# Keeping the first norm's token tiles in on-chip memory through the memory attention

## The chip, the cores and the metric

The kernel runs on one core of a Trainium2 chip. Its engines work side by side, each on its own list of instructions, in the order of that list: TensorE (in the profile PE; its weight loads PEld) multiplies matrices, VectorE (DVE) and ScalarE (ACT) do element-wise work and may read the accumulators of TensorE, GpSimd (POOL) does element-wise work between on-chip buffers, and SyncE (SP) issues nearly all transfers between the on-chip memory and the main memory. The metric is the device time of one execution, in microseconds, smaller being better.

## The reference

One layer of an encoder over 1024 tokens of width 1024, with three sub-layers, each closed by a residual and a layer norm. What the kernel must compute is `h`, with `DEPTH = 1`:

```
h = layer_norm(x, ln_in_w, ln_in_b)
h = layer_norm(ALPHA * h + hybrid_mixer(h, ...), ln1_w, ln1_b)       # first norm
h = layer_norm(ALPHA * h + memory_xattn(h, mem, ...), ln2_w, ln2_b)  # memory attention
h = layer_norm(ALPHA * h + conv_ffn(h, ...), ln3_w, ln3_b)
```

The mixer is an mLSTM over half of the width and a neighbourhood attention over the other half, with a common output projection. The memory attention lets every token attend, in 4 heads, to 256 memory rows: scores of the token with the keys, a softmax for each head, the sum of the values, an output projection and a bias `b_xo`. The last sub-layer is a gated convolutional feed-forward network.

## The kernel before

Tokens are worked in 8 tiles of 128 tokens by 1024 columns, 512 KB in fp32, 4,096 bytes in each of the 128 partitions. Products are made exact enough by splitting each operand into a high and a low part, and each product is three matmuls (`mm3`, lines 225 to 227).

The change lies at the seam between the mixer and the memory attention.

*The end of the mixer* (`out_half`, line 1061, called at 1309). `part0` in main memory holds, for each tile, ALPHA times the residual plus one half of the output projection plus the bias. For each tile, in the order `todo = [0, 2, 1, 3, 4, 6, 5, 7]`, `load_r` fetches these rows into a buffer `r` of the pool `wkB`, which has five (line 1071); TensorE makes the other half of the projection in two accumulators; VectorE adds them to `r` (line 1090, twice). Then `after1` (line 1295) normalizes the tile in place: statistics on VectorE (lines 238 to 242), the power -1/2 on GpSimd (line 243), a shift on VectorE (line 252), the scaling on ScalarE (line 253), times `ln1_w` on VectorE (line 1297), plus `ln1_b` on GpSimd (line 1298), and a store to `h_1` in main memory (line 1299). A tile's statistics are held behind the shift of the tile before (`hold`). `ln1_w` and `ln1_b` lie in the buffers vec0 and vec1. For the first two tiles `to_hT` (line 1265) makes the transposed fp16 halves that TensorE takes: a split on ScalarE and VectorE into `h1s` (two buffers), and two transposing transfers on SyncE into `h1T` (two buffers, line 1270).

*The memory attention*, again tile by tile. `load_r` (line 1380) fetches the tile from `h_1` into one of five buffers of the pool `rtiles`, which lies at the upper end of the on-chip memory; `to_hT` follows for the third tile on, and GpSimd adds `b_xo` to the tile (lines 1438 and 1447). `scores` (line 1385) makes the 48 matmuls of the scores (keys and query projection are already multiplied into one matrix) and the softmax into the halves `Ps`; `to_PT` (line 1410) transposes these by two transfers on SyncE (line 1415) into vec0 for even and vec1 for odd tiles (vec2 for the last); `out_d` (line 1418) makes the 48 matmuls with values and output projection, adds them to the tile (line 1426), normalizes and stores it, and `to_B` (line 1324) transposes it for the feed-forward network. The loop at line 1440 has `scores` of tile n+1, `to_PT` of n, `load_r` and `to_hT` of n+2, and `out_d` of n-1.

The order in which each engine gets its instructions is not the order of the program: a planner that simulates the time of each instruction writes the lists (`schedule_with_timeline_sim=True`), and puts the semaphores between them. Pools opened later may take the space of pools closed earlier; an instruction then waits for the last user of the tiles that it overlaps (`reuse_waits="tile"`). At the lower end of the on-chip memory the program keeps a scratch for transfers issued by GpSimd, 16,384 bytes in each partition unless it is told otherwise.

Of the kernel before, what the change touches and what calls it, by code (L numbers as in the profile page):

```python
# [8 lines left out]
F32 = mybir.dt.float32  # L9
# [8 lines left out]
D = 1024  # L18
SEQ = 1024
MEM = 256  # L20
NT = 8
FF = 2816
NFF = FF // 128
ALPHA = 2.0 ** 0.25
# [26 lines left out]
def run(gen):  # L51
    for _ in gen:
        pass
# [3 lines left out]
def encoder(ctx, tc, I, out):  # L57
    nc = tc.nc
    V, A, G, T, S = nc.vector, nc.scalar, nc.gpsimd, nc.tensor, nc.sync
# [19 lines left out]
    def bank(name):  # L79
        key = "mem" if name == "tk" else name  # L80
        turn[key] = turn.get(key, -1) + 1
        tag = SET[name][turn[key] % len(SET[name])]
        return pp.tile([128, 512], F32, name=name, tag=tag, bufs=NB[tag])
# [4 lines left out]
    def dscratch(name, shape, dt=F32):  # L88
        return dram.tile(shape, dt, name=name)

    h0_d = dscratch("h_0", [SEQ, D])
    part0_d = dscratch("part0", [SEQ, D])
    h1_d = dscratch("h_1", [SEQ, D])
    part1_d = dscratch("part1", [SEQ, D])
    h2_d = dscratch("h_2", [SEQ, D])
    mo_d = dscratch("mo", [SEQ, 512])
# [70 lines left out]
    def col(n=1):  # L167
        used[0] += n
        assert used[0] <= 96
        return sc[:, used[0] - n:used[0]]  # L170
# [32 lines left out]
    def split16(hi, lo, src, s):  # L203
        A.activation(hi, src, AF.Copy, scale=s)  # L204
        return V.scalar_tensor_tensor(lo, src, s, hi, op0=OP.mult, op1=OP.subtract)  # L205
# [11 lines left out]
    def slot(tag):  # L217
        return (xp.tile([128, 4096], F32R, name=tag + "h", tag=tag + "h"),
                xp.tile([128, 4096], F32R, name=tag + "l", tag=tag + "l"))
# [4 lines left out]
    def mm3(ps, lh, ll, rh, rl, first, last, skip=False):  # L224
        T.matmul(ps, lh, rh, start=first, stop=False, skip_group_check=skip)  # L225
        T.matmul(ps, lh, rl, start=False, stop=False, skip_group_check=skip)  # L226
        return T.matmul(ps, ll, rh, start=False, stop=last, skip_group_check=skip)  # L227
# [54 lines left out]
    with ExitStack() as ca:  # L282

        yml = None
        with ExitStack() as cm:
# [258 lines left out]
            with ExitStack() as c2:  # L544
# [256 lines left out]
                with ExitStack() as c1:  # L801
# [10 lines left out]
                    for c in range(4):  # L812
                        w, ic = cw[2 + c]
# [244 lines left out]
            return [wload(I[wname][(k0 + k) * 128:(k0 + k + 1) * 128, :], 1, 1024, engs[k], raws[k])  # L1058
                    for k in range(4)]

        def out_half(w, y, res, dst, work, name, after=None, bias=None, rbufs=3, early=False, alpha=ALPHA, todo=range(NT)):


            rs = {}

            def load_r(tt):
                if tt == 0 and early:
                    rs[tt] = wp.tile([128, WP], F32, name="wraw", tag="wraw", bufs=2)[:, :D]
                else:
                    rs[tt] = work.tile([128, D], F32, name="r", tag="r", bufs=rbufs)  # L1070
                S.dma_start(rs[tt], res[tt * 128:(tt + 1) * 128, :])

            load_r(todo[0])
            yield 0
            for n, tt in enumerate(todo):
                if n + 1 < NT:
                    load_r(todo[n + 1])
                r = rs.pop(tt)
                for ch in range(2):
                    ps = bank(name)  # L1080
                    for k in range(4):
                        yh, yl = y(k, tt)
                        wh, wl = w[k]
                        cc = slice(ch * 512, ch * 512 + 512)
                        mm3(ps, yh, yl, wh[:, 0, cc], wl[:, 0, cc], k == 0, k == 3)
                    rc = r[:, ch * 512:ch * 512 + 512]
                    if bias is not None:
                        V.scalar_tensor_tensor(rc, rc, alpha, ps, op0=OP.mult, op1=OP.add)
                    else:
                        V.tensor_tensor(rc, ps, rc, OP.add)  # L1090
                    yield 1
                if bias is not None:
                    G.tensor_tensor(r, r, bias, OP.add)
                if dst is not None:
                    S.dma_start(dst[tt * 128:(tt + 1) * 128, :], r)
                if after is not None:
                    yield from after(tt, r)

        wA = out_w("w_mix_out", 0, (None, V, None, V))
        yna = tuple(t.rearrange("p (k t) -> p k t", k=4) for t in slot("X2"))  # L1100

        with ExitStack() as cn:
# [109 lines left out]
            def ylk(y):  # L1212
                return lambda k, tt: (y[0][:, k, tt * 128:(tt + 1) * 128], y[1][:, k, tt * 128:(tt + 1) * 128])

            wB = []
# [17 lines left out]
    with ExitStack() as cb_:  # L1233
# [26 lines left out]
        todo = [0, 2, 1, 3, 4, 6, 5, 7]  # L1260
        rs, hT, probs, rq, holds, stores = {}, {}, {}, [], [], []
        cC = ExitStack()
        ck = cC.enter_context(tc.tile_pool(name="wkC", bufs=1, reuse_waits="tile"))

        def to_hT(ck, n, r):
            hT[n] = ck.tile([128, 2, 8, 128], F16, name="h1T", tag="h1T", bufs=2)
            hl = ck.tile([128, 2, D], F16, name="h1s", tag="h1s", bufs=2)
            split16(hl[:, 0], hl[:, 1], r, s1)
            for i in range(2):
                S.dma_start_transpose(hT[n][:, i], hl[:, i])  # L1270

        with ExitStack() as cB:
            wk = cB.enter_context(tc.tile_pool(name="wkB", bufs=1, reuse_waits="tile"))
            lw, lb = vec(0, "ln1_w"), vec(1, "ln1_b")
            p1, s1 = pow2(ln_bound(lw, lb)[1], 14)

            cs_, ncs = col(), col()
            V.tensor_scalar(cs_, p1, scales["q"][0], 2.0 ** -23, op0=OP.mult, op1=OP.mult)
            V.tensor_tensor(cs_, cs_, pk, OP.mult)
            V.tensor_scalar(ncs, cs_, -1.0, None, op0=OP.mult)  # L1280
            bxo = vec(2, "b_xo")

            wb2 = small.tile([128, 16], F32, name="wb2")
            S.dma_start(wb2, I["ln2_c"])
            bup = small.tile([128, 2 * NFF], F32, name="bup")
            S.dma_start(bup, I["b_up"])
            m2 = col(3)
            V.tensor_reduce(m2[:, 0:1], wb2[:, 0:8], axis=mybir.AxisListType.X, op=OP.max, apply_absolute_value=True)
            V.tensor_reduce(m2[:, 1:2], wb2[:, 8:16], axis=mybir.AxisListType.X, op=OP.max, apply_absolute_value=True)
            V.scalar_tensor_tensor(m2[:, 2:3], m2[:, 0:1], float(D) ** 0.5, m2[:, 1:2], op0=OP.mult, op1=OP.add)  # L1290
            ph, sh = scale_of(m2[:, 2:3], 12)
            V.tensor_scalar(wb2, wb2, sh, None, op0=OP.mult)
            holds = []

            def after1(tt, r):
                holds.append(ln_tile(r, None, None, small, hold=holds[-1] if holds else None))
                V.tensor_tensor(r, r, lw, OP.mult)
                G.tensor_tensor(r, r, lb, OP.add)
                S.dma_start(h1_d[tt * 128:(tt + 1) * 128, :], r)
                if tt in todo[:2]:  # L1300
                    first.append(r)
                    if tt == todo[1]:
                        to_hT(ck, 0, first[0])
                if tt == todo[4]:
                    to_hT(ck, 1, first[1])
                yield 1

            first = []
            run(out_half(wB, ylk(yna), part0_d, None, wk, "out", after1, rbufs=5, todo=todo))

        rtx = ExitStack()
        rt = rtx.enter_context(tc.tile_pool(name="rtiles", bufs=1, side="right", reuse_waits="tile"))

# [61 lines left out]
        Bop["B22"] = tuple(wp.tile([128, 2048], F16, name=t, tag=t, bufs=5).rearrange("p (k t) -> p k t", k=4)  # L1377
                           for t in ("whi", "wlo"))

        def load_r(n):  # L1380
            if n < NT:
                rs[n] = rt.tile([128, D], F32, name="r", tag="r", bufs=5)
                S.dma_start(rs[n], h1_d[todo[n] * 128:todo[n] * 128 + 128, :])

        def scores(ck, n):
            t = hT.pop(n)
            P = ck.tile([128, D], F32, name="P", tag="P", bufs=1)
# [46 lines left out]

        V.tensor_scalar(bxo, bxo, 1.0 / ALPHA, None, op0=OP.mult)
        for n in range(2):
            load_r(n)
            G.tensor_tensor(rs[n], rs[n], bxo, OP.add)
        P = scores(ck, 0)
        for n in range(NT - 1):  # L1440
            Pn = scores(ck, n + 1)
            to_PT(P, n)
            P = Pn
            if n + 2 < NT:
                load_r(n + 2)
                to_hT(ck, n + 2, rs[n + 2])
                G.tensor_tensor(rs[n + 2], rs[n + 2], bxo, OP.add)
            if 0 < n < NT - 2:
                run(out_d(n - 1))
# [26 lines left out]
        class Units:  # L1476
# [26 lines left out]
            def home(self, v):  # L1503
                i = v % 4
                if i not in homes:
                    homes[i] = (lambda: in_yp("Yh"), in_ur, lambda: in_yp("Yl"), in_wp)[i]()
                return homes[i]
# [88 lines left out]
        with ExitStack() as cE:  # L1596
            wk = cE.enter_context(tc.tile_pool(name="wkE", bufs=1, reuse_waits="tile"))
# [182 lines left out]
        with ExitStack() as cF:  # L1780
            wk = cF.enter_context(tc.tile_pool(name="wkF", bufs=1, reuse_waits="tile"))
# [12 lines left out]
            for j in range(1, 5):  # L1794
                for tt in range(NT):
# [3 lines left out]
                    if tt in (0, 4) and j < 4:  # L1799
                        f = 4 * j + 4 + tt // 2  # L1800
# [19 lines left out]
            rs = {}  # L1820
# [9 lines left out]
            for tt in range(NT):  # L1830
                load_r(tt + 2)
                r = rs.pop(tt)
# [8 lines left out]
                n = 256 if last else 512  # L1841
# [95 lines left out]
```

## Time and profile before

| | |
|---|---|
| median of 3 runs | 1527.25 us (1524.54 to 1528.09) |
| the profiled execution | 1526.06 us |
| its span | 1524.1 us |
| its mean granted TensorE clock | 0.985 |
| TensorE busy | 1447.8 us |
| VectorE, ScalarE, GpSimd busy | 1033.7, 825.6, 574.5 us |
| moved between the memories | 217.00 MB |
| transfers of tiles between `h` scratches and `r` buffers | 19 loads and 16 stores of 512 KB |

All lines below are of the one profiled execution. Its order of time gives, for each instruction, the start in us from the beginning of the span, the duration, the engine, the line of the kernel, the operation, output and inputs by the names of the tiles, the count where neighbours are merged, and in brackets the time for which the engine stood idle before it, with what ended that. SPq is SyncE's queue: its rows are the issues of transfers, not the transfers. A line can be that of a helper (225 to 227 are all matmuls of split products, 204 and 205 all splits), so tiles tell the stage: `out` is the end of the mixer, `S` the scores and the outputs of the memory attention.

### The profile page before, as it was taken

Reading aid. Unit: us, or ns where it says so; the run is one execution under the profiler, and the core shown is the slowest. Engines: PE = TensorE matmul, PEld = TensorE weight load, DVE = VectorE, ACT = ScalarE, POOL = GpSimd, SP = SyncE. Lnnn points to the kernel's source line nnn. Section 1 sums busy time; section 2 is a strip of 40 time slices with the busy share of each in tenths; the row PEclk is TensorE's granted clock in tenths of the full one; section 3 lists DMA queues with packets and bytes.
Section 4 is the critical chain, followed back from the end, with each engine's and each line's share of the span. In section 5 each row is a group of like instructions: output and inputs, shape, how many; then the busy total and the mean of one; then the engine's idle time right before and its main releaser. Section 6 shows DMA issues by size and latency. Waiting matters only on the chain. (4 is left out here: it accounts for less than half of the span.)

```text
span 1524.1 us, 21708 instructions
## 1 busy us (share of the span) xinstructions
PE 1447.8 (95%) x8060; PEld 869.3 (57%) x8060; DVE 1033.7 (68%) x1945; ACT 825.6 (54%) x1393; POOL 574.5 (38%) x453
## 2 busy tenths in 40 slices
PE   8999999999999898994999979999999999999998
PEld 6998776466666887861444434444444444444444
DVE  7868866536776678565456778887787779807434
ACT  5765565654544666323444758777777767503000
POOL 5442367204326766044013374434443420300543
PEclk9999999999999999997999989999999999999999
DMA  8846563315446534476333342323222436712111
GB/s 305 325 157 218 178 194 137 96 50 153 130 133 191 184 105 152 188 221 166 89 77 85 126 152 111 111 111 124 112 111 111 152 124 221 264 54 86 53 74 65
DMA packets 118687, 217.00 MB, mean 142 GB/s; under 512 B 40883, under 2 KB 69811, under 8 KB 115254
## 3 DMA queue, kind: packets, MB, share of 16 engines
q1 hardware_dynamic: 118288, 214.86, 42.3%
q8 instruction: 63, 1.03, 0.3%
q0 software_dynamic: 144, 0.49, 0.2%
q14 instruction: 42, 0.34, 0.1%
q10 hardware_dynamic: 150, 0.27, 0.0%
HBM read 158.34 MB, written 49.35 MB: 136 GB/s over the span
## 5 line engine op out<-in xcount | busy, mean ns | idle before, releaser
L1527 POOL TENSOR_TENSOR wraw<-ur 128x512 f32<-128x512 f32 x22 | 45.9, 2086 | 207.7 <-issue 192.4
L226 PE MATMUL dn<-wlo,yp 128*128 128x512 f16 (+1 forms) x284 | 105.1, 370 | 0.0
L225 PE MATMUL dn<-whi,yp 128*128 128x512 f16 (+1 forms) x284 | 104.9, 370 | 0.0
L227 PE MATMUL dn<-whi,yp 128*128 128x512 f16 (+1 forms) x284 | 104.4, 370 | 0.0
L1615 DVE SCALAR_TENSOR_TENSOR cbuf<-C,wdw,cbuf 128x1024 f32<-128x1024 f32 x44 | 69.9, 1588 | 35.3 <-ACT cbuf L1614 35.1
L227 PEld LDWEIGHTS <-wlo 128*128 128x128 f16 x540 | 52.8, 98 | 56.6 <-DVE wlo L205 1.3
L226 PEld LDWEIGHTS <-whi 128*128 128x128 f16 x540 | 52.9, 98 | 56.0 <-issue 3.2
L225 PEld LDWEIGHTS <-whi 128*128 128x128 f16 x540 | 52.9, 98 | 53.2 <-ACT whi L204 0.3
L243 POOL TENSOR_TENSOR lnrs<-lnrs,mhalf 128x1 f32<-128x1 f32 x32 | 24.8, 775 | 138.5 <-DVE lnrs L242 132.8
L205 DVE SCALAR_TENSOR_TENSOR wlo<-wraw,us,whi 128x1024 f16<-128x1024 f32 (+1 forms) x48 | 62.7, 1324 | 18.7 <-ACT whi L204 18.7
L253 ACT ACTIVATE r<-r,lnrs 128x1024 f32<-128x1024 f32 x19 | 23.6, 1240 | 88.1 <-DVE lnrs L252 88.0
L1616 DVE SCALAR_TENSOR_TENSOR cbuf<-C,wdw,cbuf 128x1024 f32<-128x1024 f32 x44 | 70.4, 1600 | 0.7
L225 PE MATMUL S<-whi,vec 128*128 128x512 f16 x128 | 49.3, 385 | 15.6 <-DMA vec<-Ps 15.6
L204 ACT ACTIVATE whi<-wraw,us 128x1024 f16<-128x1024 f32 (+1 forms) x48 | 51.2, 1103 | 16.5 <-DVE us L177 15.6
L1614 ACT ACTIVATE cbuf<-C,bdw,wdw 128x1024 f32<-128x1024 f32 x44 | 54.2, 1234 | 8.9 <-DVE C L1652 8.4
L226 PEld LDWEIGHTS <-yp 128*128 128x128 f16 x370 | 36.2, 98 | 39.9
L225 PEld LDWEIGHTS <-yp 128*128 128x128 f16 x370 | 36.2, 98 | 39.8
L227 PEld LDWEIGHTS <-yp 128*128 128x128 f16 x370 | 36.2, 98 | 39.7
L225 PE MATMUL tk<-whi,Bo 128*128 128x256 f16 (+1 forms) x192 | 53.3, 277 | 1.6 <-DVE stage L205 1.6
L227 PE MATMUL tk<-whi,Bo 128*128 128x256 f16 (+1 forms) x192 | 53.3, 278 | 0.0
L226 PE MATMUL tk<-wlo,Bo 128*128 128x256 f16 (+1 forms) x192 | 53.3, 278 | 0.0
L226 PE MATMUL tk<-wlo,Be 128*128 128x256 f16 (+1 forms) x192 | 52.4, 274 | 0.9 <-DVE wlo L205 0.9
(520 smaller groups left out, 4898.7 us busy)
## 6 DMA issues: line engine op xcount, KB each, us to landing
ur<-in_w_up_dram SPq DMA_DIRECT2D x22, 1024.0 KB
sv<-in_w_down_dram SPq DMA_DIRECT2D x22, 512.0 KB
y<-cbuf SPq DMA_DIRECT2D x22, 512.0 KB
ur<-y SPq DMA_DIRECT2D x11, 1024.0 KB
wraw<-in_w_down_dram SPq DMA_DIRECT2D x22, 512.0 KB
r<-h SPq DMA_DIRECT2D x19, 512.0 KB
h<-r SPq DMA_DIRECT2D x16, 512.0 KB
wraw<-in_w_tok_dram SPq DMA_DIRECT2D x10, 512.0 KB
```

Source lines behind the costliest of these rows:

```text
L204: A.activation(hi, src, AF.Copy, scale=s)
L205: return V.scalar_tensor_tensor(lo, src, s, hi, op0=OP.mult, op1=OP.subtract)
L225: T.matmul(ps, lh, rh, start=first, stop=False, skip_group_check=skip)
L226: T.matmul(ps, lh, rl, start=False, stop=False, skip_group_check=skip)
L227: return T.matmul(ps, ll, rh, start=False, stop=last, skip_group_check=skip)
L243: G.tensor_tensor(rs[:, 0:1], rs[:, 0:1], mhalf[:, 0:1], OP.pow)
L253: A.activation(r, r, AF.Identity, scale=rs[:, 0:1], bias=rs[:, 1:2])
L1527: G.tensor_tensor(S1, A21, A22, OP.add)
L1614: A.activation(c, C[:, 1:SEQ + 1], AF.Identity, scale=wdw[:, 1, j:j + 1], bias=bdw[:, j:j + 1])
L1615: V.scalar_tensor_tensor(c, C[:, 0:SEQ], wdw[:, 0, j:j + 1], c, op0=OP.mult, op1=OP.add)
L1616: V.scalar_tensor_tensor(c, C[:, 2:SEQ + 2], wdw[:, 2, j:j + 1], c, op0=OP.mult, op1=OP.add)
```

## The change

Eight tiles `r0` to `r7` of the pool `rtiles`, which is now opened before the end of the mixer, take the rows of `part0` (`home`). They are normalized there, and the memory attention works on the same tiles. The store to `h_1`, the loads from it, `h_1` itself and the pool `wkB` go. The third to eighth tile's `to_hT` stays where it was in the program. The scratch for transfers issued by GpSimd is made 4,096 bytes a partition.

```diff
-    h1_d = dscratch("h_1", [SEQ, D])
...
-        def out_half(w, y, res, dst, work, name, after=None, bias=None, rbufs=3, early=False, alpha=ALPHA, todo=range(NT)):
+        def out_half(w, y, res, dst, work, name, after=None, bias=None, rbufs=3, early=False, alpha=ALPHA, todo=range(NT), home=None):
...
                 if tt == 0 and early:
                     rs[tt] = wp.tile([128, WP], F32, name="wraw", tag="wraw", bufs=2)[:, :D]
+                elif home is not None:
+                    rs[tt] = home(tt)
                 else:
                     rs[tt] = work.tile([128, D], F32, name="r", tag="r", bufs=rbufs)
                 S.dma_start(rs[tt], res[tt * 128:(tt + 1) * 128, :])
...
+        rtx = ExitStack()
+        rt = rtx.enter_context(tc.tile_pool(name="rtiles", bufs=1, side="right", reuse_waits="tile"))
+
+        def home(tt):
+            n = todo.index(tt)
+            rs[n] = rt.tile([128, D], F32, name=f"r{n}")
+            return rs[n]
+
         with ExitStack() as cB:
-            wk = cB.enter_context(tc.tile_pool(name="wkB", bufs=1, reuse_waits="tile"))
...
                 G.tensor_tensor(r, r, lb, OP.add)
-                S.dma_start(h1_d[tt * 128:(tt + 1) * 128, :], r)
-                if tt in todo[:2]:
-                    first.append(r)
-                    if tt == todo[1]:
-                        to_hT(ck, 0, first[0])
+                if tt == todo[1]:
+                    to_hT(ck, 0, rs[0])
                 if tt == todo[4]:
-                    to_hT(ck, 1, first[1])
+                    to_hT(ck, 1, rs[1])
                 yield 1
 
-            first = []
-            run(out_half(wB, ylk(yna), part0_d, None, wk, "out", after1, rbufs=5, todo=todo))
-
-        rtx = ExitStack()
-        rt = rtx.enter_context(tc.tile_pool(name="rtiles", bufs=1, side="right", reuse_waits="tile"))
+            run(out_half(wB, ylk(yna), part0_d, None, None, "out", after1, todo=todo, home=home))
...
-        def load_r(n):
-            if n < NT:
-                rs[n] = rt.tile([128, D], F32, name="r", tag="r", bufs=5)
-                S.dma_start(rs[n], h1_d[todo[n] * 128:todo[n] * 128 + 128, :])
-
...
         for n in range(2):
-            load_r(n)
             G.tensor_tensor(rs[n], rs[n], bxo, OP.add)
...
             if n + 2 < NT:
-                load_r(n + 2)
                 to_hT(ck, n + 2, rs[n + 2])
                 G.tensor_tensor(rs[n + 2], rs[n + 2], bxo, OP.add)
...
-    nc = bacc.Bacc("TRN2", target_bir_lowering=False, num_devices=1)
+    nc = bacc.Bacc("TRN2", target_bir_lowering=False, num_devices=1, dynamic_dma_scratch_size=4096)
```

## The prediction, made before the changed kernel was built or run

> **What bounds the kernel now.** I read the page first, then the stretches around the lines that the diff touches, then the waits of TensorE there, and last the order of time of each queue.
>
> ```profile
> span 1524.1 us, 21708 instructions
> PE 1447.8 (95%) x8060; PEld 869.3 (57%) x8060; DVE 1033.7 (68%) x1945; ACT 825.6 (54%) x1393; POOL 574.5 (38%) x453
> ```
>
> TensorE is busy 95% of the span, so a saving counts only where it closes a hole of TensorE. The windows show one hole in the stage of the change:
>
> ```profile
> 680.00:720.00 40.00, 20.78 (x88) 8.59 (x87) 26.09 (x46) 13.27 (x28) 16.20 (x9) 0.83 0.54 163
> 760.00:800.00 40.00, 40.00 (x195) 19.16 (x194) 22.21 (x48) 18.29 (x43) 6.20 (x4) 1.00 0.40 79
> ```
>
> From 680 to 720 us TensorE works 20.78 us of 40, and its granted clock drops to 0.83; from 760 to 800 it works all 40. Its matmuls in order of time (start, duration; in brackets the idle time before, and what ended it):
>
> ```profile
> 687.07 0.38 PE L227 MATMUL S<-kq,h1T 128*128 128x512 f16 x1
> ...
> 703.07 0.61 PE L225 MATMUL S<-whi,vec 128*128 128x512 f16 x1 [15.62 <-DMA vec<-Ps]
> ...
> 703.90 0.63 PE L225 MATMUL S<-whi,vec 128*128 128x512 f16 x1
> 704.33 0.63 PE L226 MATMUL S<-wlo,vec 128*128 128x512 f16 x1
> ...
> 717.58 0.39 PE L225 MATMUL S<-kq,h1T 128*128 128x512 f16 x1 [2.40 <-DMA h1T<-h1s]
> ...
> 719.82 0.52 PE L227 MATMUL S<-kq,h1T 128*128 128x512 f16 x1 [1.20 <-DMA h1T<-h1s]
> ...
> 741.16 0.38 PE L227 MATMUL S<-kq,h1T 128*128 128x512 f16 x1
> 741.38 0.38 PE L225 MATMUL S<-whi,vec 128*128 128x512 f16 x1
> ```
>
> I call the 48 score matmuls of tile n (S<-kq,h1T) sc n, the 48 of its output (S<-whi,vec) out n; n counts in the order of the list todo. TensorE does sc0, sc1, waits 15.62 us, does out0, waits 2.40 and 1.20, does sc2 and sc3, and starts out1 at 741.38. At full rate one matmul takes 741.38 - 741.16 = 0.22 us (0.216 over many); behind the hole the step is 704.33 - 703.90 = 0.43. The SyncE queue says why (issues; a merged row spans its waits):
>
> ```profile
> 654.22 0.53 SPq L1071 DMA_DIRECT2D r<-part  x1
> ...
> 673.30 21.48 SPq L1299 DMA_DIRECT2D h<-r  x4
> 699.83 2.60 SPq L1415 DMA_TRANSPOSE vec<-Ps  x2
> ...
> 706.44 2.75 SPq L1383 DMA_DIRECT2D r<-h  x5
> 714.49 6.06 SPq L1270 DMA_TRANSPOSE h1T<-h1s  x4
> ```
>
> Two separate things are late. **PT0**, the transposed probabilities that out0 needs, is issued at 699.83 although its source was written earlier: its target is the vec0 buffer, which holds ln1_w until the eighth norm tile has been multiplied by it (L1297). **h1T of tile 2**, which sc2 needs, is issued at 714.49 behind the loads of h_1 at 706.44. The norm chain on VectorE:
>
> ```profile
> 644.44 0.21 DVE L252 TENSOR_SCALAR lnrs<-lnmv,lnrs 128x1 f32<-128x1 f32 x1
> ...
> 646.01 1.18 DVE L1297 TENSOR_TENSOR r<-r,vec 128x1024 f32<-128x1024 f32 x1
> ...
> 650.27 0.21 DVE L252 TENSOR_SCALAR lnrs<-lnmv,lnrs 128x1 f32<-128x1 f32 x1 [1.82 <-POOL lnrs L243]
> ...
> 651.60 1.27 DVE L205 SCALAR_TENSOR_TENSOR h1s<-r,sc,h1s 128x1024 f16<-128x1024 f32 x1
> ...
> 658.00 1.29 DVE L1090 TENSOR_TENSOR r<-out,r 128x512 f32<-128x512 f32 x2 [3.26 <-DMA r<-part]
> 659.20 0.20 DVE L252 TENSOR_SCALAR lnrs<-lnmv,lnrs 128x1 f32<-128x1 f32 x1
> ...
> 666.90 1.29 DVE L1090 TENSOR_TENSOR r<-out,r 128x512 f32<-128x512 f32 x2 [3.85 <-PE out L227]
> 668.11 0.20 DVE L252 TENSOR_SCALAR lnrs<-lnmv,lnrs 128x1 f32<-128x1 f32 x1
> ...
> 673.82 0.21 DVE L252 TENSOR_SCALAR lnrs<-lnmv,lnrs 128x1 f32<-128x1 f32 x1 [2.90 <-POOL lnrs L243]
> ...
> 680.99 0.20 DVE L252 TENSOR_SCALAR lnrs<-lnmv,lnrs 128x1 f32<-128x1 f32 x1
> ...
> 696.02 0.21 DVE L252 TENSOR_SCALAR lnrs<-lnmv,lnrs 128x1 f32<-128x1 f32 x1
> ...
> 698.57 1.23 DVE L1297 TENSOR_TENSOR r<-r,vec 128x1024 f32<-128x1024 f32 x1 [0.76 <-ACT r L253]
> ```
>
> One L252 ends the statistics of one tile. The first step, 644.44 to 650.27, is the undisturbed one, 5.83 us; the eighth tile comes at 696.02, and 698.57 + 1.23 = 699.80 is when vec0 comes free.
>
> **The change, part by part.**
>
> **1. Stores and loads of h_1 go** (8 of L1299, 8 of L1383). In the steady part they cost nothing, since TensorE is full there (760 to 800 row). At the start they are why sc2 is late: the split of tile 2 could not begin before its load. Now its buffers decide: the score buffer h1T has two slots, and tile 2's comes free when sc0 ends, 10.4 us (48 x 0.216) before sc1's end at 687.07 + 0.22 = 687.29, so at 676.9. Two transposes are 2.60 us of issue and 3.24 from first issue to first matmul (699.83 to 703.07): h1T of tile 2 can land near 680.5, seven us before sc1 ends. sc2 then fills 687.29 to 697.7, if SyncE issues these transposes ahead of PT0's. The order of the queues is written by a planner that fills idle queues with whatever is ready; it has put the scaling of b_xo, far down the program at L1435, at 502.6:
>
> ```profile
> L1435 DVE TENSOR_SCALAR vec<-vec x1: 694/694/694, 502.6 to 502.6; 128x1024 f32<-128x1024 f32 x1
> ```
>
> I therefore take this order as the likely one.
>
> The **ceiling** of the gain: out0, sc2 and sc3 are 144 matmuls, 31.1 us at full rate; they take 741.38 - 687.29 = 54.1. So at most 23.0 us, of which 15.62 + 2.40 + 1.20 = 19.2 are idle and 3.8 the slow clock.
>
> **2. Eight buffers in place of five for the rows of part0.** The sixth load is issued at 654.22 because it waits for the first buffer; VectorE stands 3.26 us at 658.00 and 3.85 at 666.90 for such rows. (The row names TensorE for the second, but an L1090 in order behind a load of the same kind fits as well; both readings stay open; if it is TensorE, the chain below is 3.6 us later, inside the bounds of part 3.) Without the waits: tile 2's L252 comes when its power is there,
>
> ```profile
> 647.33 2.39 POOL L1298 TENSOR_TENSOR r<-r,vec 128x1024 f32<-128x1024 f32 x1 [2.92 <-DVE lnrs L242]
> 649.68 0.56 POOL L243 TENSOR_TENSOR lnrs<-lnrs,mhalf 128x1 f32<-128x1 f32 x1
> ...
> 657.10 0.55 POOL L243 TENSOR_TENSOR lnrs<-lnrs,mhalf 128x1 f32<-128x1 f32 x1
> ...
> 676.64 2.34 POOL L1298 TENSOR_TENSOR r<-r,vec 128x1024 f32<-128x1024 f32 x1 [2.86 <-DVE lnrs L242]
> ```
>
> 657.10 + 0.55 = 657.7 in place of 659.20. The next step, with a split like that of 651.60 in it, I put at 6.8 (between 5.83 and the 7.4 from 650.27 to 657.7): 664.5 for 668.11. Then 5.8 as from 668.11 to 673.82: 670.3. The step to 680.99 is 7.17 with the two adds of the last tile in it; I take 5.9, so 676.2. The last two together took 696.02 - 680.99 = 15.0, shared with the softmax of sc0 and sc1, which stays: 691.2. L1297 starts 2.55 later and runs 1.23: vec0 free at **695.0** for 699.8, and out0 could start at 695.0 + 3.27 = 698.3, just behind sc2.
>
> **3. What moves into this time.** Splits of tiles 2 to 4 and the adds of b_xo (L1438, L1447) now find their tiles ready while the chain still runs. A split in the chain cost 7.4 - 5.83 = 1.55 in the second step. An add on GpSimd takes 2.34 (L1298 is the same operation). It fits the 2.92 us in which GpSimd waits in each step; but VectorE suffers beside it:
>
> ```profile
> 677.26 1.75 DVE L1397 TENSOR_SCALAR mn<-mn,sc 128x2 f32<-128x2 f32 x1
> ```
>
> This operation on two columns ends at 679.01, as the add that began at 676.64 does (678.98). L1297 is ready 1.6 us after the power (644.44 to 646.01), so an add put right behind the power would hold it 2.35 - 1.6 = 0.75. Bounds: nothing, if neither falls into the chain, and 3 x 1.55 + 5 x 0.75 = 8.4 if three splits and five adds do. A gain is excluded, as this is added work. I take half, **4.2**: PT0 usable at 702.5, a hole of 702.5 - 697.7 = 4.8, and behind it 8 matmuls at 0.43 (as from 703.07) instead of 0.22, 1.7.
>
> The Trainium skill, SBUF — State Buffer, section SBUF: two separate sides, calls the port pair of GpSimd and VectorE an exclusive lock, held for a whole instruction, also against VectorE operations with two SBUF inputs. The row above agrees for a scalar operation; none here shows L1297 held. By that rule every add that starts first holds L1297 as priced; without it the adds would cost nothing and the sum would be 2 us lower.
>
> **4. The smaller scratch.** One transfer is issued by GpSimd, the masks:
>
> ```profile
> L1105 POOL DMA_DIRECT2D vec<-in_na_mask_dram x1: 757/757/757, 369.0 to 369.0; - x1
> ...
> 472.40 7.42 POOL L1160 TENSOR_TENSOR tb<-vec,vec 128x256 f32<-128x256 bf16 x9
> ```
>
> Issued at 369.0, needed at 472.40: 103 us of cover. I take nothing; if the transfer took longer than the cover, each us more would show at 472. Its 12,288 bytes a partition are what the three more tiles need, so no other buffer shrinks. The convolution buffers opened later overlap the token tiles, as they overlapped the five slots; they now lie over the first five tiles, which are done first, so no wait is added there.
>
> **5. Carrying to the end.** From out1 on TensorE is full, and the next stage hangs on this one:
>
> ```profile
> 835.81 0.76 SPq L1415
> ...
> 836.74 5.41 DMA ur<-in_w_up_dram
> ```
>
> The first load of w_up goes out right behind the last transposes of probabilities, into buffers that these free. So I carry the gain whole.
>
> **Sum**, against the profiled execution's own 1526.06 us: -23.0 + 4.8 + 1.7 = -16.5, **1509.5**. The median shown, 1527.25, is 1.2 above that execution; I forecast **1510** for a median.
>
> **Rivals.**
>
> *No hole is left.* Splits and adds fall outside the chain, out0 follows sc2 at once: the whole ceiling less the 0.6 between 697.7 and 698.3, 1503.7, with the median's offset 1505. For it: VectorE has 14 us free of 40 from 680 to 720. Against: the softmax is in the same stretch.
>
> *PT0 is put ahead of h1T of tile 2 on SyncE.* Then both wait for vec0. TensorE stands from 687.29 to 702.5, 15.2, and 1.7 of slow clock: gain 6.1, 1520 (1521 as a median). For it: the program writes PT0's transposes first, and the queue is in order. Against: the planner's habit above.
>
> *Slower:* the same order, and a chain that ends later than now. The place is L1297 of the eighth tile; the price is a us for each us; it decides from out0 at 708.6 (741.38 - 31.1 - 1.7), that is vec0 free after 705.3. It gets there if five adds go ahead of L1298 at their full 2.35 and three splits cost 1.55: 695.0 + 11.8 + 4.7 = 711.5, out0 at 714.8, 6 us slower, 1532. Against: the chain has the older work, which a planner serves first.
>
> *The tiles help, but nothing shows:* the same order with vec0 free between 702 and 708, within 3 us of now.
>
> **How the numbers follow.** Forecast 0.46 (1506 to 1514), no hole 0.24, PT0 first 0.14, nothing shows 0.07, slower 0.09. 0.2%, 3 us, is about what a measurement tells from no change. Faster 0.46 + 0.24 + 0.14 = 0.84. The range takes in the no-hole case with 3 us for a planner that orders later stages otherwise, and PT0 first: 1501 to 1522.
>
> **What would show it.** TensorE does sc2 right behind sc1, and the wait on vec<-Ps falls from 15.6 to under 7; the transposes of tile 2 are issued near 677 on SyncE; no L1090 waits for part0's rows; the last L1297 ends between 695 and 704. A wait on vec<-Ps still over 12 with out0 ahead of sc2 would make the forecast wrong, as would a new hole after 830.

## The result, and the profile after

The changed kernel takes **1513.46 us**, the median of four runs (1512.1 to 1515.13), beside 1525.89 us (1524.3 to 1528.09) of four runs of the kernel before on the same chip. The ratio is 0.9918, with a 95% interval of 0.9899 to 0.9937: 12.4 us, or 9.6 to 15.4, are gained. The forecast was 1510, in a range of 1501 to 1522.

The head of the page of the changed kernel (span; busy time of each engine; what was moved):

```profile
span 1510.5 us, 21655 instructions
...
PE 1444.8 (96%) x8060; PEld 867.4 (57%) x8060; DVE 1038.1 (69%) x1945; ACT 824.9 (55%) x1393; POOL 575.0 (38%) x453
...
DMA packets 116383, 208.61 MB, mean 138 GB/s; under 512 B 40627, under 2 KB 69555, under 8 KB 112950
```

The span falls by 13.6 us (1524.1 - 1510.5) and the engines do the same work as before; 8.4 MB less are moved (217.00 - 208.61), which is 16 transfers of 512 KB.

The two stretches of the changed kernel that the prediction compared (busy time and count of PE, PEld, DVE, ACT, POOL, then the granted clock, the DMA share and GB/s):

```profile
680.00:720.00 40.00, 30.85 (x131) 13.27 (x130) 31.74 (x51) 19.12 (x40) 20.36 (x10) 0.87 0.35 60
760.00:800.00 40.00, 40.00 (x195) 19.18 (x194) 21.12 (x47) 18.33 (x43) 5.86 (x4) 1.00 0.33 66
```

TensorE now works 30.85 of the 40 us from 680 to 720, where it worked 20.78. The hole is smaller, but there is one still. TensorE of the changed kernel round it, in order of time:

```profile
701.62 0.38 PE L225 MATMUL S<-kq,h1T 128*128 128x512 f16 x1
711.15 0.61 PE L224 MATMUL S<-whi,vec 128*128 128x512 f16 x1 [9.15 <-DMA vec<-Ps]
711.55 0.63 PE L225 MATMUL S<-wlo,vec 128*128 128x512 f16 x1
711.98 0.63 PE L224 MATMUL S<-whi,vec 128*128 128x512 f16 x1
...
716.59 0.38 PE L224 MATMUL S<-whi,vec 128*128 128x512 f16 x1
...
730.84 0.38 PE L224 MATMUL S<-whi,vec 128*128 128x512 f16 x1
```

The three waits of 15.62, 2.40 and 1.20 us have become one of 9.15. Behind it thirteen matmuls run at 0.43 us a step: 716.59 - 711.15 = 5.44 where 13 x 0.216 = 2.8, so 2.6 us are lost to the slow clock. out1 starts at 730.84 in place of 741.38. The stage begins 0.5 us later here (the first shift, `lnrs<-lnmv,lnrs`, of the norm chain is at 644.97 in place of 644.44), so the stage gains 10.5 + 0.5 = 11.0 us. From out1's start to the end the profiled executions take 782.8 us before and 779.7 after; over all ten profiled kernels of this case that stretch lies between 779.7 and 782.8 us, so what the kernel gains beyond the stage can't be told from the spread.

SyncE's issues in the changed kernel, in order of time, a merged row spanning its waits:

```profile
630.73 3.93 SPq L1072 DMA_DIRECT2D r<-part  x8
...
677.67 12.97 SPq L1271 DMA_TRANSPOSE h1T<-h1s  x4
707.92 2.60 SPq L1411 DMA_TRANSPOSE vec<-Ps  x2
```

All eight loads of part0 go out at once. The transposes of tile 2 go out at 677.67, and ahead of PT0's: TensorE does sc2 right behind sc1. PT0's are issued at 707.92 in place of 699.83. That is what the hole now waits for, and it is *later* than before. VectorE's norm chain in the changed kernel shows why:

```profile
644.97 0.21 DVE L251 TENSOR_SCALAR lnrs<-lnmv,lnrs 128x1 f32<-128x1 f32 x1
...
646.54 1.19 DVE L1305 TENSOR_TENSOR r<-r,vec 128x1024 f32<-128x1024 f32 x1
...
650.81 0.21 DVE L251 TENSOR_SCALAR lnrs<-lnmv,lnrs 128x1 f32<-128x1 f32 x1 [1.83 <-POOL lnrs L242]
...
652.14 1.27 DVE L204 SCALAR_TENSOR_TENSOR h1s<-r,sc,h1s 128x1024 f16<-128x1024 f32 x1
...
654.04 2.92 DVE L1305 TENSOR_TENSOR r<-r,vec 128x1024 f32<-128x1024 f32 x1
...
660.01 0.21 DVE L251 TENSOR_SCALAR lnrs<-lnmv,lnrs 128x1 f32<-128x1 f32 x1 [1.78 <-POOL lnrs L242]
...
669.17 0.21 DVE L251 TENSOR_SCALAR lnrs<-lnmv,lnrs 128x1 f32<-128x1 f32 x1 [1.74 <-POOL lnrs L242]
...
704.85 3.05 DVE L1305 TENSOR_TENSOR r<-r,vec 128x1024 f32<-128x1024 f32 x1
```

and GpSimd beside it, where L1433 and L1441 are the adds of b_xo and L1306 the add of ln1_b:

```profile
647.86 2.40 POOL L1306 TENSOR_TENSOR r<-r,vec 128x1024 f32<-128x1024 f32 x1 [2.92 <-DVE lnrs L241]
...
653.48 2.40 POOL L1433 TENSOR_TENSOR r<-r,vec 128x1024 f32<-128x1024 f32 x1 [2.70 <-DVE h1s L204]
...
662.68 2.41 POOL L1433 TENSOR_TENSOR r<-r,vec 128x1024 f32<-128x1024 f32 x1 [2.71 <-DVE h1s L204]
...
704.47 2.34 POOL L1441 TENSOR_TENSOR r<-r,vec 128x1024 f32<-128x1024 f32 x1 [4.11 <-DVE h1s L204]
```

The product with ln1_w (L1305) takes 1.19 us at 646.54 and 2.92 at 654.04. The second ends at 654.04 + 2.92 = 656.96, 1.08 after the end of GpSimd's add (653.48 + 2.40 = 655.88). So the product's own duration holds a wait of about 1.75 for the add. The steps of the chain are 9.20 and 9.16 (650.81, 660.01, 669.17); the last product ends at 704.85 + 3.05 = 707.90, and PT0 is issued 0.02 later. One number sums the chain up, and does not depend on when the stage begins: from the first shift to the end of the last product it is 707.90 - 644.97 = **62.9 us** here and 699.80 - 644.44 = 55.4 before.

### The profile page after: what moved, and what is told of

The parts are those of the page before. It is cut to its first block, busy times and chain, and to the rows that moved or that the text cites. A ratio compares the mean times of both kernels' runs of the same rounds, so it can differ in the third digit from the quotient of the medians.

```text
span 1510.5 us, 21655 instructions
## 1 busy us (share of the span) xinstructions
PE 1444.8 (96%) x8060; PEld 867.4 (57%) x8060; DVE 1038.1 (69%) x1945; ACT 824.9 (55%) x1393; POOL 575.0 (38%) x453
## 2 busy tenths in 40 slices
DMA packets 116383, 208.61 MB, mean 138 GB/s; under 512 B 40627, under 2 KB 69555, under 8 KB 112950
## 5 line engine op out<-in xcount | busy, mean ns | idle before, releaser
L204 DVE SCALAR_TENSOR_TENSOR wlo<-wraw,us,whi 128x1024 f16<-128x1024 f32 (+1 forms) x48 | 62.7, 1323 | 18.7 <-ACT whi L203 18.7
L252 ACT ACTIVATE r<-r,lnrs 128x1024 f32<-128x1024 f32 x19 | 23.5, 1239 | 72.3 <-DVE lnrs L251 72.2
L224 PE MATMUL tk<-whi,Bo 128*128 128x256 f16 (+1 forms) x192 | 53.3, 277 | 1.6 <-DVE stage L204 1.6
L226 PE MATMUL tk<-whi,Bo 128*128 128x256 f16 (+1 forms) x192 | 53.3, 278 | 0.0
```

The costliest lines, as they stand in the source:

```text
L252: A.activation(r, r, AF.Identity, scale=rs[:, 0:1], bias=rs[:, 1:2])
```

## The experiments

The theory from these rows: the kept tiles did what they were meant to (loads early, sc2 early), and GpSimd's adds of b_xo, which now find their tiles ready, hold VectorE's products with ln1_w and so vec0, and so out0. The rivals: that splits and not adds lengthen the chain; that something else than vec0 keeps out0; that the stores and the scratch matter. All ratios are to runs of the kernel before that were taken beside them: 1525.46 us (19 runs) for the first four experiments, 1527.63 us (7 runs) for the other four.

### The scratch alone

The kernel before with the smaller scratch and nothing else:

```diff
-    nc = bacc.Bacc("TRN2", target_bir_lowering=False, num_devices=1)
+    nc = bacc.Bacc("TRN2", target_bir_lowering=False, num_devices=1, dynamic_dma_scratch_size=4096)
```

> The kernel before, with only the scratch for transfers of GpSimd made 4,096 bytes a partition. Theory (the scratch costs and gives nothing; the masks have over 100 us of cover): within 3 us of the kernel before, the same 15.6 us hole of TensorE before the first output product. Rival (part of the 12.4 us gained comes from the smaller scratch or from all buffers lying 12,288 bytes lower): 2 to 12 us faster.

It took 1526.1 us, ratio 1.0002 (0.9989 to 1.0015). The waits of TensorE in this run, from 640 to 760 us (what waited, for what; total, times, longest):

```profile
PE S L225 <- DMA vec<-Ps: 15.8, 1, 15.8
PE S L225 <- DMA h1T<-h1s: 2.3, 1, 2.3
PE S L227 <- DMA h1T<-h1s: 1.2, 1, 1.2
PE out L225 <- DVE r L1090: 1.1, 1, 1.1
```

The three waits of before stand as they were; the fourth row belongs to the end of the mixer, and the kernel before has it too, just ahead of 640 us. The scratch costs and gains nothing.

### Eight buffers, and still the way through h_1

The kernel before with the small scratch and eight buffers for part0's rows; stores and loads of h_1 stay.

```diff
-            run(out_half(wB, ylk(yna), part0_d, None, wk, "out", after1, rbufs=5, todo=todo))
+            run(out_half(wB, ylk(yna), part0_d, None, wk, "out", after1, rbufs=8, todo=todo))
```

> The kernel before with the small scratch and eight buffers in place of five for the rows of part0; the tiles are still stored to h_1 and loaded again, into five buffers. Theory (the buffers alone shorten the chain of norms, vec0 free near 695 in place of 699.8; the loads of h_1 still come before the transposes of tile 2): no addition of the output product to the tile waits for part0's rows, hole 10 to 11 us in place of 15.6, 3 to 6 us faster than before. Rival (the buffers were no limit, the row at 666.9 waited for TensorE): under 2 us faster.

It took 1520.67 us, ratio 0.9972 (0.996 to 0.9983), a gain of 4.8 between the medians. The profile is of its fastest run, 1516.88 us. Its norm chain, first shift, a wait of a sum, and last product; then TensorE behind the hole; then SyncE:

```profile
643.27 0.21 DVE L252 TENSOR_SCALAR lnrs<-lnmv,lnrs 128x1 f32<-128x1 f32 x1
...
662.85 0.69 DVE L1090 TENSOR_TENSOR r<-out,r 128x512 f32<-128x512 f32 x1 [1.25 <-PE out L227]
...
691.36 1.21 DVE L1297 TENSOR_TENSOR r<-r,vec 128x1024 f32<-128x1024 f32 x1
```

```profile
695.88 0.61 PE L225 MATMUL S<-whi,vec 128*128 128x512 f16 x1 [9.61 <-DMA vec<-Ps]
```

```profile
699.15 2.84 SPq L1383 DMA_DIRECT2D r<-h  x5
707.38 6.13 SPq L1270 DMA_TRANSPOSE h1T<-h1s  x4
```

The chain is 692.57 - 643.27 = 49.3 us long, for 55.4 before: 6.1 us off the chain is what the buffers for part0 are worth by themselves. (The smaller scratch alone left the chain at 55.4.) sc2 stays late, since its tile is loaded at 699.15. The sums wait for TensorE 1.25 us where before it was 3.85: the long wait was chiefly the buffers'.

### The adds held back

The changed kernel with every add of b_xo put behind the last tile's add of ln1_b in GpSimd's list; the work is the same.

```diff
+            last_lb = [None]
...
-                G.tensor_tensor(r, r, lb, OP.add)
+                last_lb[0] = G.tensor_tensor(r, r, lb, OP.add)
...
-            G.tensor_tensor(rs[n], rs[n], bxo, OP.add)
+            with tc.issue_after(last_lb[0].ins):
+                G.tensor_tensor(rs[n], rs[n], bxo, OP.add)
...
-                G.tensor_tensor(rs[n + 2], rs[n + 2], bxo, OP.add)
+                with tc.issue_after(last_lb[0].ins):
+                    G.tensor_tensor(rs[n + 2], rs[n + 2], bxo, OP.add)
```

> The changed kernel, with the adds of b_xo on GpSimd held behind the last norm tile's add of ln1_b. Theory (five of these adds stand in the chain of norms and hold VectorE's product with ln1_w, 2.9 us in place of 1.2): the products with ln1_w are back at 1.2 us, vec0 comes free 7 to 10 us sooner than 707.9, the hole of 9.15 us falls under 3, 7 to 10 us faster than the changed kernel, near 1505. Rival (the splits of tiles 2 to 4 on VectorE stretch the chain, not the adds): hole still over 6 us, under 3 us faster than the changed kernel.

It took **1501.94 us** (1501.3 to 1503.39), ratio 0.9853 (0.9831 to 0.9875): 23.5 us less than before, and 11.5 less than the changed kernel (1513.46). Its stretch from 680 to 720 us, its norm chain, and the first matmul of out1:

```profile
680.00:720.00 40.00, 40.00 (x187) 17.86 (x185) 36.92 (x54) 16.86 (x37) 24.87 (x12) 1.00 0.43 73
```

```profile
644.80 0.21 DVE L251 TENSOR_SCALAR lnrs<-lnmv,lnrs 128x1 f32<-128x1 f32 x1
...
653.87 1.17 DVE L1306 TENSOR_TENSOR r<-r,vec 128x1024 f32<-128x1024 f32 x1
...
696.88 1.22 DVE L1306 TENSOR_TENSOR r<-r,vec 128x1024 f32<-128x1024 f32 x1
```

```profile
718.88 0.38 PE L224 MATMUL S<-whi,vec 128*128 128x512 f16 x1
```

The product beside which the add ran takes 1.17 again. The chain is 698.10 - 644.80 = 53.3 us long, 9.6 less than with the adds in it. TensorE has no hole left among these matmuls, and its clock is 1.00 in each 40 us from 640 to 760; out1 starts 22.5 us earlier than before, in a stage that begins 0.36 later. So the whole ceiling of 23.0 is there, and the adds had been taking half of it. The gain of 11.5 us is more than the 7 to 10 expected.

### The probabilities elsewhere

The changed kernel with PT0 and PT1 in the two buffers `wraw`, which hold nothing at that time, so that out0 does not wait for vec0. The adds stay in the chain.

```diff
-            t = f16(vecs.tile([128, D], F32, name=f"vec{i}", tag=f"vec{i}")).rearrange(
-                "p (n k t) -> p n k t", n=2, k=8)
+            t = (wp.tile([128, WP], F32, name="wraw", tag="wraw", bufs=2)[:, :D] if n < 2 else
+                 vecs.tile([128, D], F32, name=f"vec{i}", tag=f"vec{i}"))
+            t = f16(t).rearrange("p (n k t) -> p n k t", n=2, k=8)
```

> The changed kernel, with the transposed probabilities of the first two tiles written to the two weight staging buffers, which are idle there, in place of vec0 and vec1. Theory (out0 waits only because vec0 holds ln1_w until the end of the chain of norms): its transposes go out as soon as the softmax of tile 0 is split (near 696), the 9.15 us hole goes, 8 to 11 us faster than the changed kernel, near 1504. Rival (the softmax or SyncE's order is as late as the chain): the wait moves to another place of the same stage, under 3 us faster.

It took 1504.18 us (1503.39 to 1505.58), ratio 0.9867 (0.9845 to 0.989). The issue of PT0, the end of the chain, and TensorE behind the rest of the hole:

```profile
694.77 3.22 SPq L1412 DMA_TRANSPOSE wraw<-Ps  x2
```

```profile
703.89 1.23 DVE L1305 TENSOR_TENSOR r<-r,vec 128x1024 f32<-128x1024 f32 x1 [1.00 <-ACT r L252]
```

```profile
700.00 0.39 PE L226 MATMUL S<-whi,wraw 128*128 128x512 f16 x1 [0.66 <-DMA wraw<-Ps]
```

PT0 is issued nine us before the last product begins, and the hole is 0.66 us, though the chain of norms is still 59.6 us long. So the probabilities were ready, and out0 waited for vec0 alone.

### Both remedies, and splits held back

Two kernels ask whether anything is left. One has both remedies; the other holds the adds, and besides it the splits of the fourth tile on (behind the last product with ln1_w):

```diff
-                to_hT(ck, n + 2, rs[n + 2])
+                with (tc.issue_after(last_lw[0].ins) if n else nullcontext()):
+                    to_hT(ck, n + 2, rs[n + 2])
```

> The changed kernel with the adds of b_xo held and the first two tiles' transposed probabilities in the weight staging buffers. Theory (with the adds held TensorE has no hole left in this stage, so the two remedies do not add up): within 3 us of the kernel with the adds held alone, 1499 to 1505. Rival (each closes a loss of its own): 1490 to 1496.

> The changed kernel with the adds of b_xo held as in the run before, and also VectorE's splits of the fourth to eighth tile held behind the last product with ln1_w. Theory (what is left of the chain's lengthening, vec0 free at 698.1 where the prediction's sum without added work has 695.0, is the splits): vec0 free between 694 and 697; the time is that of the kernel with the adds held alone or up to 4 us more, since that had no hole left and the fourth tile's scores now come later. Rival (the splits lie beside the chain): vec0 still free at 698 or later.

Both remedies together took 1504.13 us (1502.95 to 1505.5), ratio 0.985 (0.9835 to 0.9865): not to be told from the adds held alone, 0.9853. They close the same hole and don't add up. The kernel with the splits held took 1503.62 us in its one run, so its time says no more than that. Its chain says what splits cost:

```profile
646.31 0.21 DVE L251 TENSOR_SCALAR lnrs<-lnmv,lnrs 128x1 f32<-128x1 f32 x1
...
694.93 1.21 DVE L1306 TENSOR_TENSOR r<-r,vec 128x1024 f32<-128x1024 f32 x1
```

696.14 - 646.31 = 49.8 us, 3.5 less than with the adds alone held: three splits left the chain, those of tiles 3 to 5, 1.2 us each. The split of tile 2 is still in it.

### Stores back

The changed kernel with the eight stores to `h_1` put back, which nobody reads:

```diff
+    h1_d = dscratch("h_1", [SEQ, D])
...
+                S.dma_start(h1_d[tt * 128:(tt + 1) * 128, :], r)
```

> The changed kernel with the eight stores of the normalized tiles to h_1 put back; nothing reads them. Theory (the stores lie in SyncE's idle time and beside TensorE's work; prediction, part 1): within 3 us of the changed kernel, hole 9 to 10 us. Rival (stores that wait for GpSimd's add of ln1_b hold up the transposes behind them on SyncE): 3 to 10 us slower than the changed kernel, and transposes of tile 2 or of the first probabilities later by as much.

It took 1514.02 us (1511.73 to 1515.53), ratio 0.9918 (0.9901 to 0.9934), as the changed kernel. On SyncE the transposes of tile 2 go out at 677.70 us and PT0's at 709.00, for 677.67 and 707.92 in the changed kernel; the hole is 8.5 us, a little under the 9 to 10 expected. The chain is 1.5 us longer, 64.5, but 27 matmuls of sc3 stand ahead of out0 in place of 17. So the stores cost nothing that the time shows.

### The adds on VectorE

The changed kernel with all adds of b_xo on VectorE, in the same places: they stay in the chain, and only GpSimd's hold goes.

```diff
-            G.tensor_tensor(rs[n], rs[n], bxo, OP.add)
+            V.tensor_tensor(rs[n], rs[n], bxo, OP.add)
...
-                G.tensor_tensor(rs[n + 2], rs[n + 2], bxo, OP.add)
+                V.tensor_tensor(rs[n + 2], rs[n + 2], bxo, OP.add)
```

> The changed kernel with all adds of b_xo on VectorE in place of GpSimd, free to be put anywhere. Theory (a GpSimd add holds VectorE's product with ln1_w until it ends; without it only the adds' own 1.2 us each stand in the chain): no product with ln1_w over 1.3 us beside an add, vec0 free between 700 and 705 in place of 707.9, hole 2 to 7 us, 3 to 8 us faster than the changed kernel. Rival (any work put into the chain costs the same; GpSimd's hold is not the cause): hole over 8 us and no gain.

It took 1508.93 us (1507.39 to 1509.91), ratio 0.988 (0.9865 to 0.9895). The first shift of its chain, a product and an add, the last product, and TensorE behind the hole:

```profile
645.66 0.21 DVE L251 TENSOR_SCALAR lnrs<-lnmv,lnrs 128x1 f32<-128x1 f32 x1
...
663.03 1.22 DVE L1305 TENSOR_TENSOR r<-r,vec 128x1024 f32<-128x1024 f32 x1
664.16 1.22 DVE L1433 TENSOR_TENSOR r<-r,vec 128x1024 f32<-128x1024 f32 x1
...
702.20 1.22 DVE L1305 TENSOR_TENSOR r<-r,vec 128x1024 f32<-128x1024 f32 x1
```

```profile
706.72 0.43 PE L224 MATMUL S<-whi,vec 128*128 128x512 f16 x1 [3.38 <-DMA vec<-Ps]
```

The product takes 1.22 and the add itself 1.22, less than the 1.75 by which GpSimd's add held the product. The hole is 3.38 in place of 9.15, and the kernel is 4.5 us faster than the changed one. The chain is 703.42 - 645.66 = 57.8 us long: of the 9.6 us that the adds cost on GpSimd, 5.1 are gone and 4.5 remain (in one of the adds GpSimd's hold is still there: at 672.51 us it takes 3.00). So GpSimd's hold makes the adds dearer, about twice as dear, but work in the chain costs on VectorE too; holding the adds back is worth 7 us more (1508.93 to 1501.94).

## Why the prediction was right, and where it was wrong

The forecast case came: the order on TensorE and SyncE, and the last wait, were the ones that it named, and the time lies 3.5 us above it.

| step | predicted | measured |
|---|---|---|
| part 1: h1T of tile 2 issued, ahead of PT0 | near 677 | 677.67 |
| part 1: sc2 right behind sc1 | yes | yes |
| part 1: ceiling of the stage | 23.0 | 22.9 (adds held) |
| part 1: stores cost | 0 | nothing seen (ratio 0.9918 with and without) |
| part 2: chain without added work | 50.6 (695.0 - 644.44) | 49.3 (eight buffers alone) |
| part 3: splits and adds in the chain | 4.2, at most 8.4 | 13.6 (62.9 - 49.3) |
| hole | 4.8 | 9.15 |
| slow clock behind it | 1.7 | 2.6 |
| part 4: scratch | 0 | 0 (1.0002) |

**Part 1** held in each point. The gain of its early loads and early sc2 was all there, but could only be seen whole once the adds were out of the way.

**Part 2** held within 1.3 us. Which of its two readings of the 3.85 us wait was right is answered too: in the run with eight buffers alone the sums wait for TensorE 0.5 and 1.25 us, so most of it was the buffers.

**Part 3 is the step that failed**, in size and not in kind. It took half of 3 x 1.55 + 5 x 0.75 = 8.4, so 4.2. The chain with the added work is 62.9 us long, and 49.3 without it: 13.6 us, more than even the upper bound. Each chain is read from one execution (55.4 us both before and with the scratch alone). Splits and adds come apart by two more differences of chains:

- The *adds* cost 62.9 - 53.3 = 9.6 us, where at most 3.75 were allowed.
- The *splits* cost 53.3 - 49.3 = 4.0 us, within the 4.65 allowed, though four of them stood in the chain and not three: 3.5 for tiles 3 to 5 (53.3 - 49.8) and 0.5 for tile 2.

So the term that failed is the add at 0.75. It came from "an add put right behind the power", which would have been 1.6 us ahead of the product. But the program writes a tile's split ahead of its add, and the add overwrites what the split reads, so no add can start before the split has ended; and on VectorE the split stands just ahead of the product of the next tile. GpSimd's row says so: 653.48, [2.70 <-DVE h1s L204], 2.70 us behind the power and 0.56 ahead of the product. So the hold is 1.75 instead of 0.75.

Nor was it five adds but six that began before vec0 came free (the last at 704.47). Beside four of them a product took 2.88 to 3.05 us, beside one it took 2.06 (at 683.14), and one held splits of the softmax. Had the add been placed by its own dependency, 6 x 1.75 = 10.5 would have come out beside the measured 9.6. And "half" had no ground: the planner fills an idle GpSimd with whatever is ready, the very habit on which part 1 relied, so the end of the bounds, not their middle, was to be taken; even that would have been too low.

The rule cited in part 3, from the Trainium skill, SBUF — State Buffer, section SBUF: two separate sides, said that the port pair is an exclusive lock for a whole instruction, and against a VectorE operation with two SBUF inputs too. The trace agrees now for the product itself: 1.17 us without an add, 2.92 with one.

**What softened it.** The prediction let TensorE stand from the end of sc2, 697.7. The planner had put 17 matmuls of sc3 ahead of out0 (the last at 701.62), which fill 3.7 us of the hole. Thus out0 started 8.65 us later than predicted (711.15 for 702.5), but the hole grew by only 4.4. The prediction hadn't counted on that.

That the time lies only 3.5 us above the forecast is partly luck. The stage gained 11.0 of the 16.5 us of the sum, 5.5 less. But the kernel before took 1525.89 us beside this run, 1.4 below the 1527.25 from which the forecast was counted, and 1.4 of the 12.4 us gained lie outside the stage.

**The rivals.** PT0 did not go ahead of h1T. "No hole" did not come with this change, and the kernel with the adds held is that case: 1501.9 for the 1505 given to it. The two cases "slower" and "nothing shows" were **worked out wrongly**: they let the whole 31.1 us of out0, sc2 and sc3 follow out0's start, though in the order that they assume sc2 is done before it. With 96 matmuls left, 20.7 us, a loss begins not from out0 at 708.6 but from 741.38 - 20.7 - 1.7 = 719.0. By the wrong figure this kernel, whose out0 starts at 711.15, would be slower than before; it is 12 us faster. The slower case's own out0, 714.8, gives out1 at 714.8 + 1.7 + 20.7 = 737.2, 4 us sooner than before and not 6 later. Both cases had too high a chance, and with little effect on the range.

**Carrying.** The stage gained 11.0 and the kernel 12.4 (9.6 to 15.4), and the stretch behind out1 is not longer than before (779.7 us for 782.8): no hole opened later that ate it.

## What to carry to other kernels

When a change lets work start earlier, price it in the place where its own dependencies first allow it to run, next to what it then meets; a planner that fills idle engines will put it there, urgent or not. Element-wise work on GpSimd is not free because GpSimd is idle: look which VectorE operations with two on-chip inputs run beside it, and whether they are on the chain that sets the end; holding such work back until the chain is through gave here 11.5 us of 1513. And when a rival case moves an operation ahead, take that operation out of the sum of what is left.

## What the runs showed of the hardware

In these traces a VectorE operation that GpSimd holds shows the wait inside its own duration and not as idle time before it: the same product is 1.17 and 2.92 us long. The sign is an end about one undisturbed duration after the end of GpSimd's instruction (656.96 and 655.88, 1.08 us apart).

The hold works in the other direction too. With the adds on VectorE, GpSimd's add of ln1_b that starts beside one takes longer than its 2.40 us:

```profile
655.82 1.21 DVE L1433 TENSOR_TENSOR r<-r,vec 128x1024 f32<-128x1024 f32 x1
```

```profile
655.97 3.33 POOL L1306 TENSOR_TENSOR r<-r,vec 128x1024 f32<-128x1024 f32 x1 [4.51 <-DVE r L1305]
```

Beside a row of adds, VectorE gets one held operation through for each add. In the kernel with the adds held, four splits of VectorE meet four adds of GpSimd (merged rows, x4):

```profile
705.08 10.12 DVE L204 SCALAR_TENSOR_TENSOR Ps<-P,mn,Ps 128x256 f16<-128x256 f32 x4
```

```profile
705.10 9.81 POOL L1444 TENSOR_TENSOR r<-r,vec 128x1024 f32<-128x1024 f32 x4
```

Four such splits took 1.68 us elsewhere in the same run (from 693.31); here they took 10.12. Taken one by one they last 2.65, 2.56, 2.57 and 2.56 us, and each ends 0.28 to 0.29 us after the end of an add, so the two engines take turns: each split pays for a whole add. That cost nothing there, as TensorE had other matmuls, but it says that held-back work should not be let go all at once into a chain.

The slow clock behind a hole of TensorE doesn't grow with the hole: eight matmuls at the slow step behind 15.62 us, thirteen behind 9.15, nine behind the 8.5 with the stores back, eight behind the 3.38 with the adds on VectorE, none behind 0.66. The Trainium skill, TensorE: Matmul & The Clock Gate, section What's actually happening, says that the clock follows a free-running window, so that the number of slow matmuls differs from run to run; these counts fit that, and no run here was made to test it.
